# A hybrid decoder step: the samples get a mixer and queries of their own, and every weight split moves to VectorE

## The chip, the core and the metric
The kernel runs on one core of one Trainium2 chip. The metric is the device time of one execution in microseconds (us), the median of three runs. Engines are called as in the profile: PE (TensorE matmul; PEld its weight loads), DVE (VectorE), ACT (ScalarE), POOL (GpSimd), SP (SyncE, which issues transfers). An instruction of an engine starts in the order of that engine's program, when the semaphores it waits for allow it.

## The reference
Two layers over 512 prompt tokens (one sequence) and 64 sample tokens (8 sequences of 8 steps, with state carried in). D is 1024. Each layer is a mixer and an expert retrieval:

```
hn = modulate(rmsnorm(x, norm1), sh1, sc1)          # shift and scale by sequence, from c @ w_ada
xa, bg, cg, xs, ga, gb = split(hn @ w_in, 6)        # six parts of 1024 columns
ya = rglru(conv4(xa)); yb = bg * conv3(cg * xs)     # gated scan over time, short convolution
x += g1 * ((sigmoid(ga) * ya + sigmoid(gb) * yb) @ w_out)
hn2 = modulate(rmsnorm(x, norm2), sh2, sc2)
q = (hn2 @ w_q).reshape(t, 8 heads, 2, 128)
s = einsum('thpd,hpkd->thpk', q, sub_keys)          # 128 scores in each half
sv, si = top_k(s, 16)                               # 16 x 16 sums of a head, of which the best 16:
fv, fi = top_k(sv[:, :, 0, :, None] + sv[:, :, 1, None, :], 16)
idx = si[.., 0] * 128 + si[.., 1] at fi             # one of 16384 experts
g = softmax(fv)
x += g2 * sum_k g_k * gelu(u_tab[idx_k] . hn2) * v_tab[idx_k]
```

Outputs: the normed x of prompt and samples, and the last convolution inputs and scan states. All is float32.

## The kernel before
Channels lie on the partitions, tokens along the free axis: x is 8 channel tiles of 128 x 576, the prompt's 512 columns first. Weights stream as blocks of 128 x 1024 float32 (512 KB), two to a load (`load_pair`, L144, on SP's queue, six raw buffers). To get float32 out of the faster float32r matmuls, each block is cut in two by `split_blk` (L130): ACT copies it to `hi`, and `lo = raw - hi` is a subtraction (L141) on DVE or POOL; four buffers of each. A product is three passes: hi by hi, hi by lo, lo by hi, 24 weight loads for 8 channel tiles. A running sum of `pool_share` decides who subtracts: of the u blocks beside the gates POOL takes all (SHARE_A = 1.0), of the u and v blocks of the product stage every other one (SHARE_B = 0.5), of wq every other one, of w_in and w_out none.

The stages of a layer:
- *Mixer* (`mixer_in`, L342): for each channel tile c six products (`proj`), 48 blocks, over all 576 tokens. Such a product is two matmuls of 256 and 320 columns for each weight load, into the two banks of a `big` tile of PSUM (`mm_tokens`, L152). Convolutions, gates, scan and merge follow on DVE and ACT, in separate operations for prompt and samples. In layer 1 the modulation chunks (`ada`, fp32 matmuls L189) stand between the blocks. Then w_out, 8 blocks.
- *Queries* (`queries`, L663): wq's 16 blocks over all tokens; scores; top-k on DVE (`topk_half`, `combine`).
- *Gates and first activations* (`phase_a`, L774): 384 prompt tokens, the dense ones, meet every expert on PE. Their gates become matrices: DVE writes one-hot rows (`oh`, L794; `A`, L800), PE multiplies them (`pgm`, L805), ACT evicts, and the pieces go to DRAM. Beside this, NA = 80 of the 128 u blocks are multiplied (`pu`, L512); 64 of their activations wait in DRAM (`ad`), 16 in SBUF.
- *Products* (`phase_b`, L844): 128 v blocks are multiplied by activation x gate (`pvo`, L870), and the other 48 u blocks (`ub`) between them. DVE multiplies activation and gate (L900) and splits the result (`wl`, L903).
- *Gathered tokens*: the other 128 prompt tokens and the 64 samples, in NG = 3 groups of 64, fetch their experts' rows by indirect transfers that POOL issues (L520): 192 rows of u and 192 of v a layer, each 128 x 1024. DVE makes a dot of each u row (`ur`, L526) and adds each v row times its weight (`acc`, L543). `pump` emits these steps at rates of the work beside them: 0.3 a us of the queries' vector work, 0.5 of the gates', 1.6 to a block of the products.

The order within an engine is that of a list scheduler: priority is the place in the program, and splits and loads stand AHEAD = 2000 steps before their place (`tc.high_priority`).

Of the kernel before, what the change touches and what calls it, by code (L numbers as in the profile page):

```python
# [1040 lines left out]
```

## Time and profile before

| | |
|---|---|
| device time, three runs | 3845.72, 3853.9, 3854.32 us; median 3853.9 |
| the profiled execution | span 3846.9 us (the page gives no other time of it) |
| PE busy | 3484.8 us, 91% |
| DVE busy | 3204.7 us, 83% |
| POOL busy | 2022.2 us, 53% |
| ACT busy | 1476.0 us, 38% |
| transfers | 960.62 MB, mean 250 GB/s |

Busy shares are means over stages with different limits, so the windows below cut the span at the stages' ends: layer 1's mixer from 42 to 480 us, norm and first queries to 570, queries and gates to 1206, products to 1944; layer 2 the same from 1966 on. An operation's min, median and max show whether it always takes the same time.

### The profile page before, as it was taken

How to read it: one execution, taken by the hardware profiler on the slowest of the kernel's cores; microseconds unless marked ns; L12 is line 12 of the kernel's file. 1: busy time of each engine (PE TensorE's matmuls, PEld its weight loads, DVE VectorE, ACT ScalarE, POOL GpSimd, SP SyncE). 2: the span in 40 equal slices, each digit the busy share in tenths (PEclk: the TensorE clock that was granted, in tenths of full speed). 3: DMA queues.
4: the chain of work that ended last, by engine and by line, in shares of the span. 5: the costliest groups of instructions: out<-in, count | busy, mean ns of one | idle time of the engine just before them, and what ended most of it. 6: DMA issues, size and time to landing. Idle time of an engine off the chain costs nothing.

```text
span 3846.9 us, 57240 instructions
## 1 busy us (share of the span) xinstructions
PE 3484.8 (91%) x21120; PEld 3180.7 (83%) x21120; DVE 3204.7 (83%) x5485; ACT 1476.0 (38%) x1876; POOL 2022.2 (53%) x1360
## 2 busy tenths in 40 slices
PE   8999998776879999999989998987677899999997
PEld 6999988776768999888879998877676799998886
DVE  5444489999997999998875556999999879999888
...
GB/s 249 188 189 165 69 138 263 246 233 223 291 272 298 334 338 340 341 358 362 315 131 79 82 83 65 209 254 233 225 263 279 280 338 322 338 357 342 355 341 200
DMA packets 366712, 960.62 MB, mean 250 GB/s; under 512 B 45920, under 2 KB 149472, under 8 KB 359648
## 3 DMA queue, kind: packets, MB, share of 16 engines
...
q8 instruction: 165, 2.70, 0.3%
...
## 4 chain that ended last, share of the span: by engine, by line
PE 55%; DVE 36%; issue 4%; DMA 2%; POOL 2%; ACT 1%; SPq 0%; DVEq 0%; POOLq 0%; ACTq 0%
PE pvo L870 19%; PE pj L159 16%; PE pu L512 12%; DVE ur L526 11%; DVE oh L794 4%; DVE A L800 4%; PE po L159 3%; POOL vr L520 1%; PE pq L722 1%; PE pm L189 1%; POOL lo_v L141 1%; DVE acc L543 1%; PE pg L420 1%; DMA raw_v<-in_vtab_dram 1%; PE pt L203 1%
## 5 line engine op out<-in xcount | busy, mean ns | idle before, releaser
L520 POOL DMA_INDIRECT ur<-in_utab_dram,gidx x384 | 481.6, 1254 | 512.9 <-DVE dot L526 281.2
L520 POOL DMA_INDIRECT vr<-in_vtab_dram,gidx x384 | 540.8, 1408 | 250.5 <-DVE acc L543 173.4
L543 DVE SCALAR_TENSOR_TENSOR acc<-vr,dot,acc 128x1024 f32<-128x1024 f32 x378 | 644.6, 1705 | 10.6 <-DMA vr<-in_vtab_dram,gidx 7.2
L526 DVE CUSTOM_DVE_ANT_0 ur<-ur,xt 128x1024 f32<-128x1024 f32 x384 | 613.4, 1605 | 8.8 <-DMA ur<-in_utab_dram,gidx 8.8
L512 PE MATMUL pu<-h2h,hi_u 128*128 128x384 f32 x1280 | 454.0, 355 | 62.4 <-ACT ao L830 62.4
L870 PE MATMUL pvo<-hi_v,wh 128*128 128x512 f32 x1536 | 488.7, 392 | 0.0
L870 PE MATMUL pvo<-lo_v,wh 128*128 128x512 f32 x1536 | 477.6, 390 | 0.0
L870 PE MATMUL pvo<-hi_v,wl 128*128 128x512 f32 x1536 | 466.0, 390 | 2.4 <-DVE acc L543 1.2
L512 PE MATMUL pu<-h2h,lo_u 128*128 128x384 f32 x1280 | 452.5, 353 | 6.0 <-POOL lo_u L141 5.9
L512 PE MATMUL pu<-h2l,hi_u 128*128 128x384 f32 x1280 | 451.2, 352 | 0.0
L141 POOL TENSOR_TENSOR lo_u<-raw_u,hi_u 128x1024 fp32r<-128x1024 f32 x160 | 405.6, 2537 | 28.5 <-ACT hi_u L140 25.7
L141 POOL TENSOR_TENSOR lo_v<-raw_v,hi_v 128x1024 fp32r<-128x1024 f32 x128 | 343.8, 2686 | 65.4 <-ACT hi_v L140 63.0
L159 PE MATMUL pj<-hnl,hi_wi 128*128 128x256 f32 (+1 forms) x1536 | 343.1, 301 | 2.5 <-DVE hnl L280 2.4
L159 PE MATMUL pj<-hnh,hi_wi 128*128 128x256 f32 (+1 forms) x1536 | 339.7, 301 | 5.5 <-ACT hnh L283 4.1
L870 PEld LDWEIGHTS pvo<-hi_v,wl 128*128 128x128 f32 x1536 | 288.1, 188 | 64.2 <-DVE wl L903 1.6
L870 PEld LDWEIGHTS pvo<-lo_v,wh 128*128 128x128 f32 x1536 | 288.3, 188 | 61.3
L159 PE MATMUL pj<-hnh,lo_wi 128*128 128x256 f32 (+1 forms) x1536 | 337.7, 298 | 0.0
L870 PEld LDWEIGHTS pvo<-hi_v,wh 128*128 128x128 f32 x1536 | 285.3, 188 | 54.9 <-issue 0.4
L512 PEld LDWEIGHTS pu<-h2h,hi_u 128*128 128x128 f32 x1280 | 256.4, 200 | 65.6 <-ACT ao L830 64.9
L140 ACT ACTIVATE hi_u<-raw_u 128x1024 fp32r<-128x1024 f32 x160 | 169.7, 1061 | 317.0 <-PE pu L512 162.4
L140 ACT ACTIVATE hi_v<-raw_v 128x1024 fp32r<-128x1024 f32 x256 | 272.0, 1062 | 29.5 <-issue 13.8
L512 PEld LDWEIGHTS pu<-h2h,lo_u 128*128 128x128 f32 x1280 | 255.9, 200 | 17.9 <-POOL lo_u L141 13.8
...
## 6 DMA issues: line engine op xcount, KB each, us to landing
raw_v<-in_vtab_dram SPq DMA_DIRECT2D x256, 512.0 KB
raw_u<-in_uT_dram SPq DMA_DIRECT2D x160, 512.0 KB
...
gt<-gd SPq DMA_DIRECT2D x768, 64.0 KB
...
```

Of the source, the lines that this page charges most:

```text
L140: S.activation(hi, raw, AF.Copy)
L141: e.tensor_tensor(out=lo, in0=raw, in1=hi.bitcast(F32), op=ALU.subtract)
L159: PE.matmul(part(out, q), a[:, w], b[:, k, PARTS[q][0]:PARTS[q][1]], start=(k == 0 and a is hi and b is xh), stop=(k == KT - 1 and a is lo))
L189: PE.matmul(pm[j * 32:(j + 1) * 32, 0:256], c32[:, k, :], raw[k // 4][:, j * 256:(j + 1) * 256], start=(k < 4), stop=(k >= 4))
L203: PE.matmul(pt[:, q * 16:q * 16 + NSEQ], ms[:, q * P:(q + 1) * P], sel, start=True, stop=True)
L512: PE.matmul(pu[:, 0:TD], a[:, w], b[:, k, 0:TD], start=(k == 0 and a is hi and b is h2h), stop=(k == KT - 1 and a is lo))
L520: G.indirect_dma_start(out=rt, out_offset=None, in_=tab, in_offset=bass.IndirectOffsetOnAxis(ap=gidx[:, g, h, k:k + 1], axis=0))
L526: V.tensor_tensor_reduce(out=ur, in0=ur, in1=xt[g], scale=1.0, scalar=0.0, op0=ALU.mult, op1=ALU.add, accum_out=dot[:, g, h, k:k + 1])
L543: V.scalar_tensor_tensor(out=acc[g], in0=vr, scalar=w, in1=acc[g], op0=ALU.mult, op1=ALU.add)
L794: V.tensor_tensor(out=o, in0=iota2.unsqueeze(1).to_broadcast([P, 4, P, 2]), in1=slot(t, a, c0), op=ALU.is_equal)
L800: V.tensor_tensor(out=A[:, z], in0=oh[0], in1=slot(t, 2 + z, c0), op=ALU.mult)
L870: PE.matmul(pv[t][q], a[:, tk], b[:, q * 512:(q + 1) * 512], start=(n == 0 and a is wh and b is vh), stop=(n == P - 1 and a is wl))
```

## The change
- The products over all tokens run over the prompt's 512 columns alone, one matmul to a weight load, in one bank (`bank`, four of them).
- The samples get a generator `samples()`. It is stepped 2.5 times (layer 1) or 3 times (layer 2) beside each mixer block (`beside`, SIDE). It makes nine products (six of w_in, w_out, two of wq): the 64 tokens are the stationary operand, plain fp32 weights move in 512 columns, the two column halves to the two halves of the array. For these the weights are streamed a second time in another layout (swin, swout, swq: 72 blocks of 512 KB a layer). Convolution, gates, scan, merge, second norm, top-k and the list of rows follow over all channel tiles at once.
- When the generator is done, the samples' gathers are issued beside the mixer's blocks (MPUMP = 2.5 a block), and go on in the gates. NG falls from 3 to 2; the number of rows is the same. Beside the queries no gather is issued (QRATE 0), beside the gates 0.35 a us (0.5), beside a product block 2.9 while the u blocks run there and 1.0 after (1.6).
- All subtractions of `split_blk` are on DVE. `tc.issue_after(anchor)` puts the gather steps behind the last split in the order; it adds no wait. POOL issues gathers and little else.
- NA falls from 80 to 64: 64 u blocks stand beside the gates, 64 in the product stage; 48 activations wait in DRAM (64).
- Gate pieces are formed in quarters of 4 tokens (halves of 8), so one-hot operations have 512 elements (1024). wh and wl lie in a spare slice of h2h and h2l.
- The mixer's merged output is kept in float32 and split after the loop over c.

```diff
-NG = (T - TD) // 64
-NA = 80
+NG = (NP - TD) // 64
+NA = 64
-SHARE_A, SHARE_B = 1.0, 0.5   # of the splits, what GpSimd takes
-QRATE, ARATE, BPUMP = 0.3, 0.5, 1.6
+SIDE = (2.5, 3.0)
+MPUMP, QRATE, ARATE, BPUMP = 2.5, 0.0, 0.35, (2.9, 1.0)
-    def split_blk(raw, nm, pool_share=0.0):
+    def split_blk(raw, nm):
...
-            e.tensor_tensor(out=lo, in0=raw, in1=hi.bitcast(F32), op=ALU.subtract)
+            anchor[0] = V.tensor_tensor(out=lo, in0=raw, in1=hi.bitcast(F32), op=ALU.subtract).ins
...
-                    for q in qs:
-                        PE.matmul(part(out, q), a[:, w], b[:, k, PARTS[q][0]:PARTS[q][1]],
-                                  start=(k == 0 and a is hi and b is xh), stop=(k == KT - 1 and a is lo))
+                    PE.matmul(out[:, c0:c1], a[:, w], b[:, k, c0:c1],
+                              start=(k == 0 and a is hi and b is xh), stop=(k == KT - 1 and a is lo))
...
+    def pump(n):
+        credit[0] += n
+        while credit[0] >= 1.0 and gtasks:
+            with tc.issue_after(anchor[0]):
+                gtasks.popleft()()
+            credit[0] -= 1.0
+        credit[0] = min(credit[0], 1.0)
...
+        def beside():
+            if todo:
+                n = todo.pop(0)
+                ada(n // 24, [n % 24])
+            steps[0] += SIDE[l]
+            while steps[0] >= 1.0:
+                steps[0] -= 1.0
+                if next(chain, None) is None:
+                    steps[0] = -1e9
+            if steps[0] < -1.0:
+                pump(MPUMP)
...
-            S.activation(mgh[:, c, :], yb, AF.Copy)
-            V.tensor_tensor(out=mgl[:, c, :], in0=yb, in1=mgh[:, c, :].bitcast(F32), op=ALU.subtract)
+        for _ in chain:
+            pass
...
+        def product(src, lhs, nm, put):
+            acc = ubank(f"sa{l}_{nm}")
+            for kk in range(KT // 2):
+                raw = load_pair(src[kk], f"s{l}_{nm}_{kk}")
+                for u in range(2):
+                    k = 2 * kk + u
+                    for r in range(2):
+                        PE.matmul(acc[r * NS:(r + 1) * NS, :], lhs[:, k, :], raw[u][:, r * 512:(r + 1) * 512],
+                                  start=(k == 0), stop=(k == KT - 1))
+                yield 1
+            tm = st.tile([P, 512], F32, tag="rows", bufs=ROWS, name=f"tm{l}_{nm}")
+            S.activation(tm, acc, AF.Copy)
+            pt = small(f"spt{l}_{nm}")
+            for q in range(4):
+                PE.transpose(pt[:, q * P:(q + 1) * P], tm[:, q * P:(q + 1) * P], ident)
+            put(pt)
+            yield 1
...
+        work_of = Gathered(f"s{l}", gidx, gate, dot, {0: xt})
+        work_of.first(0, range(4))
+        work_of.second(1, lambda g, acc: finish_samples(l, mod, acc))
...
-            for half in range(2):
-                pgm = big(f"pgm{l}_{t}_{ch}_{half}")
-                c0 = ch * 16 + half * 8
+            for q in range(4):
+                c0 = ch * 16 + q * 4
...
-                hi, lo = split_blk(raw[u], f"u{l}_{i}", SHARE_A)
+                hi, lo = split_blk(raw[u], f"u{l}_{i}")
...
-                vh, vl = split_blk(vraw[u], f"v{l}_{i}", SHARE_B)
-                wh = pb.tile([P, TD], F32R, tag="wh", bufs=WB, name=f"wh{l}_{i}")
-                wl = pb.tile([P, TD], F32R, tag="wl", bufs=WB, name=f"wl{l}_{i}")
+                vh, vl = split_blk(vraw[u], f"v{l}_{i}")
+                wh, wl = (w_[:, u * TD:(u + 1) * TD] for w_ in (wht, wlt))
...
-                pump(BPUMP)
+                pump(BPUMP[i0 < NA])
```

How the order stands before and after, at three places. First PE's program in layer 1's mixer (`pj` a product of w_in, `sa` one of the samples' products, `spg` their scan gates, `pm` and `pt` the modulation). Before, each weight block meets the tokens in two parts:

```order
L159 MATMUL pj_0_2_615<-hnh,hi_wi_0_2_611 128x256
L159 MATMUL pj_0_2_615<-hnh,hi_wi_0_2_611 128x320
L159 MATMUL pj_0_2_615<-hnl,hi_wi_0_2_611 128x256
L159 MATMUL pj_0_2_615<-hnl,hi_wi_0_2_611 128x320
L159 MATMUL pj_0_2_615<-hnh,lo_wi_0_2_612 128x256
L159 MATMUL pj_0_2_615<-hnh,lo_wi_0_2_612 128x320
```

After, the place between two blocks:

```order
L150 MATMUL pj_1_1_1091<-hnh_334,hi_wi_1_1_1087 128x512
L150 MATMUL pj_1_1_1091<-hnl_335,hi_wi_1_1_1087 128x512
L150 MATMUL pj_1_1_1091<-hnh_334,lo_wi_1_1_1088 128x512
L476 MATMUL sa_gb<-raw_s_gb_1135,hs_511 64x512 x2
L537 MATMUL spg_1_777<-sxc_701,rg_3_1_347 128x64
L186 MATMUL pm_14_1049<-raw_ada_14_1045,c_121 32x256 x4
L186 MATMUL pm_14_1049<-raw_ada_14_1046,c_121 32x256 x4
L476 MATMUL sa_gb<-raw_s_gb_1136,hs_511 64x512 x2
L200 MATMUL pt_13_1060<-sel,ms_13_972 128x9 x2
L476 MATMUL sa_cg<-raw_s_cg_1155,hs_511 64x512 x2
L186 MATMUL pm_15_1120<-raw_ada_15_1116,c_121 32x256 x4
```

The pairs became single matmuls of 512 columns, and the samples' products, with the weights as the moving operand, stand between them.

Second, the gates. POOL's program before, where u blocks 50 to 54 are split (`ur` a gather):

```order
L141 TENSOR_TENSOR lo_u_50_10278<-raw_u_25_10272,hi_u_50_10277 128x1024
L520 DMA ur_0_2_7_10625<-in_utab_dram,gidx_4952 128x1024
L520 DMA ur_0_2_8_10787<-in_utab_dram,gidx_4952 128x1024
L141 TENSOR_TENSOR lo_u_51_10308<-raw_u_25_10273,hi_u_51_10307 128x1024
L520 DMA ur_0_2_9_10813<-in_utab_dram,gidx_4952 128x1024
L520 DMA ur_0_2_10_10907<-in_utab_dram,gidx_4952 128x1024
L141 TENSOR_TENSOR lo_u_52_10402<-raw_u_26_10396,hi_u_52_10401 128x1024
L141 TENSOR_TENSOR lo_u_53_10432<-raw_u_26_10397,hi_u_53_10431 128x1024
L520 DMA ur_0_2_11_10935<-in_utab_dram,gidx_4952 128x1024
L520 DMA ur_0_2_12_10943<-in_utab_dram,gidx_4952 128x1024
L141 TENSOR_TENSOR lo_u_54_10526<-raw_u_27_10520,hi_u_54_10525 128x1024
```

DVE's program after, from the split of block 53 on (`smd`, `ggd`, `t8d`, `eqd` belong to the combination of the top-k lists):

```order
L133 TENSOR_TENSOR lo_u_53_9821<-raw_u_26_9787,hi_u_53_9820 128x1024
L805 TENSOR_TENSOR eqd_2_6219<-eqd_2_6219,doff 128x2048
L819 TENSOR_SCALAR smd_2_6209<-smd_2_6209 128x8
L794 TENSOR_TENSOR t8d_2_6220<-eqd_2_6219 128x1024
L820 TENSOR_TENSOR ggd_2_6141<-exd_2_6208,smd_2_6209 128x128
L795 TENSOR_TENSOR t8d_2_6220<-t8d_2_6220 128x128x4
L809 TENSOR_TENSOR eqd_2_6219<-eqd_2_6219,dsid_2_6214 128x2048
L903 CAST ghd_2_6143<-ggd_2_6141 128x128
L796 TENSOR_TENSOR t8d_2_6220<-t8d_2_6220 128x128x2
```

and 245 rows later the next split, among the one-hots:

```order
L930 TENSOR_TENSOR oh_2_36_8961<-iota_83,sl_2_4302 128x512
L935 TENSOR_TENSOR A_2_36_8965<-oh_2_36_8961,sl_2_4302 128x512 x2
L930 TENSOR_TENSOR oh_2_40_8981<-iota_83,sl_2_4302 128x512
L133 TENSOR_TENSOR lo_u_54_9855<-raw_u_27_9850,hi_u_54_9854 128x1024
L930 TENSOR_TENSOR oh_2_40_8983<-iota_83,sl_2_4302 128x512
L935 TENSOR_TENSOR A_2_40_8985<-oh_2_40_8981,sl_2_4302 128x512 x2
L930 TENSOR_TENSOR oh_2_44_9000<-iota_83,sl_2_4302 128x512
L930 TENSOR_TENSOR oh_2_44_8998<-iota_83,sl_2_4302 128x512
L935 TENSOR_TENSOR A_2_44_9002<-oh_2_44_8998,sl_2_4302 128x512 x2
L133 TENSOR_TENSOR lo_u_55_9885<-raw_u_27_9851,hi_u_55_9884 128x1024
```

The splits moved from POOL's own list, where they alternate with gathers, into DVE's, where splits 53 and 54 are 245 rows apart.

Third, DVE in the product stage at block 92, before (`ao` activation by gate, `wl` its lower part, `ur` and `dot` a gathered dot):

```order
L141 TENSOR_TENSOR lo_ub_92_12336<-raw_ub_88_2_12330,hi_ub_92_12335 128x1024
L526 ISA ur_2_3_3_14779,dot_4954<-ur_2_3_3_14779,xt_2_5542 128x1024
L526 ISA dot_4954 128x1
L900 TENSOR_TENSOR ao_90_12174<-ao_90_12174,gt_88_12235 128x384 x2
L526 ISA ur_2_3_4_14782,dot_4954<-ur_2_3_4_14782,xt_2_5542 128x1024
L526 ISA dot_4954 128x1
L526 ISA ur_2_3_5_14812,dot_4954<-ur_2_3_5_14812,xt_2_5542 128x1024
L526 ISA dot_4954 128x1
L903 TENSOR_TENSOR wl_90_12404<-ao_90_12174,wh_90_12403 128x384
L141 TENSOR_TENSOR lo_v_90_12400<-raw_v_88_1_12395,hi_v_90_12399 128x1024
L526 ISA ur_2_3_6_14846,dot_4954<-ur_2_3_6_14846,xt_2_5542 128x1024
```

and after (`urp` a prompt token's row; `h2l` now holds what wl held):

```order
L133 TENSOR_TENSOR lo_ub_92_12136<-raw_ub_88_2_12130,hi_ub_92_12135 128x1024
L1032 TENSOR_TENSOR ao_90_11975<-ao_90_11975,gt_88_12036 128x384
L667 ISA urp_0_2_0_12093,dot_4299<-urp_0_2_0_12093,xt_0_4756 128x1024
L667 ISA dot_4299 128x1
L133 TENSOR_TENSOR lo_ub_93_12166<-raw_ub_88_2_12131,hi_ub_93_12165 128x1024
L1032 TENSOR_TENSOR ao_90_11975<-ao_90_11975,gt_88_12036 128x384
L667 ISA urp_0_2_1_12096,dot_4299<-urp_0_2_1_12096,xt_0_4756 128x1024
L667 ISA dot_4299 128x1
L1035 TENSOR_TENSOR h2l<-ao_90_11975,h2h 128x384
L133 TENSOR_TENSOR lo_v_90_12200<-raw_v_88_1_12195,hi_v_90_12199 128x1024
L667 ISA urp_0_2_2_12124,dot_4299<-urp_0_2_2_12124,xt_0_4756 128x1024
L667 ISA dot_4299 128x1
```

Every block now has its subtraction here (`lo_ub_93`, `lo_v_91`, where every other one was POOL's), and gathered dots stand right behind the splits.

## Rows read from the trace of the kernel before
**Rows 1.** The page's first lines: span, then busy us, share, instructions by engine
```profile
span 3846.9 us, 57240 instructions
...
PE 3484.8 (91%) x21120; PEld 3180.7 (83%) x21120; DVE 3204.7 (83%) x5485; ACT 1476.0 (38%) x1876; POOL 2022.2 (53%) x1360
```
**Rows 2.** The page: the chain that ended last, shares by engine
```profile
PE 55%; DVE 36%; issue 4%; DMA 2%; POOL 2%; ACT 1%; SPq 0%; DVEq 0%; POOLq 0%; ACTq 0%
```
**Rows 3.** Windows: stretch, its us, busy us (instructions) by engine, PEclk, DMA share, GB/s
```profile
42.00:480.00 438.00, 436.27 (x3447) 405.37 (x3448) 208.65 (x392) 176.70 (x248) 23.56 (x78) 0.99 0.48 156
480.00:570.00 90.00, 82.91 (x648) 74.06 (x647) 76.22 (x311) 37.12 (x68) 29.25 (x21) 0.91 0.35 121
570.00:1206.00 636.00, 494.11 (x3146) 467.86 (x3147) 621.70 (x1363) 239.84 (x255) 400.00 (x237) 0.87 0.77 259
1206.00:1944.00 738.00, 736.76 (x3539) 644.70 (x3538) 662.61 (x630) 274.92 (x365) 548.18 (x315) 1.00 0.95 339
1700.00:1800.00 100.00, 100.00 (x450) 82.78 (x449) 85.31 (x94) 37.05 (x48) 65.03 (x39) 1.00 1.00 362
1966.00:2352.00 386.00, 379.55 (x2753) 374.43 (x2753) 210.34 (x360) 169.59 (x218) 37.14 (x83) 0.98 0.24 77
2440.00:3075.00 635.00, 490.45 (x3136) 463.12 (x3135) 621.25 (x1360) 239.07 (x253) 397.93 (x237) 0.88 0.77 258
```
**Rows 4.** Waits from 570 to 1206 us: in total, times, longest
```profile
PE pgm L805 <- DVE A L800: 53.0, 49, 3.4
```
**Rows 5.** Lines, 570 to 1206: busy us, mean ns | idle before, releasers
```profile
L526 DVE CUSTOM_DVE_ANT_0 ur<-ur,xt 128x1024 f32<-128x1024 f32 x153 | 245.0, 1605 | 4.8 <-DMA ur<-in_utab_dram,gidx 4.8
...
L141 POOL TENSOR_TENSOR lo_u<-raw_u,hi_u 128x1024 fp32r<-128x1024 f32 x80 | 202.9, 2538 | 14.4 <-ACT hi_u L140 13.0
...
L805 PE MATMUL pgm<-A,oh 128*128 128x128 f16 x768 | 72.7, 250 | 53.1 <-DVE A L800 53.0
```
**Rows 6.** Each line's instructions: ns min/median/max, first and last start, forms
```profile
L543 DVE SCALAR_TENSOR_TENSOR acc<-vr,dot,acc x378: 1186/1277/3974, 1336.1 to 3815.1; 128x1024 f32<-128x1024 f32 x189
...
L526 DVE CUSTOM_DVE_ANT_0 ur<-ur,xt x384: 1192/1212/4065, 569.7 to 3198.4; 128x1024 f32<-128x1024 f32 x192
...
L141 POOL TENSOR_TENSOR lo_u<-raw_u,hi_u x160: 2346/2407/4423, 618.9 to 3069.7; 128x1024 fp32r<-128x1024 f32 x160
...
L141 DVE TENSOR_TENSOR lo_wi<-raw_wi,hi_wi x96: 1197/1224/1226, 36.2 to 2274.9; 128x1024 fp32r<-128x1024 f32 x96
...
L794 DVE TENSOR_TENSOR oh<-iota,sl x192: 674/681/5640, 960.0 to 3052.1; 128x1024 f16<-128x1024 f16 x192
```
**Rows 7.** Timeline of DVE at 3142 us: start, duration, instruction
```profile
3142.36 1.21 DVE L526 CUSTOM_DVE_ANT_0 ur<-ur,xt 128x1024 f32<-128x1024 f32 x1
...
3143.50 3.40 DVE L526 CUSTOM_DVE_ANT_0 ur<-ur,xt 128x1024 f32<-128x1024 f32 x1
...
3146.83 1.21 DVE L526 CUSTOM_DVE_ANT_0 ur<-ur,xt 128x1024 f32<-128x1024 f32 x1
```
**Rows 8.** Timeline of POOL over the same stretch
```profile
3142.91 2.91 POOL L141 TENSOR_TENSOR lo_v<-raw_v,hi_v 128x1024 fp32r<-128x1024 f32 x1
3145.96 1.77 POOL L520 DMA_INDIRECT ur<-in_utab_dram,gidx  x1
```
**Rows 9.** The chain in order of time: start, us, engine, product, line, matmuls
```profile
1186.88 49.14 PE pu L512 x283
1256.62 8.34 PE pu L512 x48
...
2035.88 38.39 PE pj L159 x288
...
3625.22 122.07 PE pvo L870 x538
```
**Rows 10.** Timeline of PE at two fp32 products of the mixer
```profile
203.83 1.07 PE L189 MATMUL pm<-raw_ada,c 128*32 128x256 f32 x16
...
2114.43 2.10 PE L420 MATMUL pg<-xc,rg 128*128 128x256 f32 x8
```

More of the change, by code (lines that the diff above doesn't have):

```diff
@@ L150, in load_pair, with mm_tokens @@
         return raw
-    def mm_tokens(out, hi, lo, xh, xl, halves=((0, 1),)):
-        for qs in halves:
+    def mm_tokens(out, hi, lo, xh, xl, parts=((0, NP),)):
+        for c0, c1 in parts:
             for k in range(KT):
@@ L359, in mixer_in, with work, load_rg @@
         SY.dma_start(bb, bufb[l])
-        def work(c, nm):
-            if nm == "yb":
-                return mx.tile([P, T], F32, tag=nm, bufs=1, name=f"{nm}{l}_{c}")
-            tag, n = ("xt", NG) if nm in ("sga", "sgb", "h") else ("rows", ROWS)
-            return st.tile([P, T], F32, tag=tag, bufs=n, name=f"{nm}{l}_{c}")
+        def work(nm, shape=(NP,)):
+            return mx.tile([P, *shape], F32, tag="w", bufs=WORK, name=f"{nm}{l}")
+        def load_rg(c, pair):
+            for t_, d_ in zip(pair, (rgwa, rgwx)):
+                for h in range(2):
+                    SY.dma_start(t_[h * 64:(h + 1) * 64, h * 64:(h + 1) * 64], d_[l, h][:, c, :])
+        chain = samples(l, vt, mod, mx, A, B, work, load_rg, rgs[2:], (ba, hz, bb), (ca_o, h_o, cb_o))
+        steps = [0.0]
+        def beside():
[9 more added lines that the diff above has]
+                pump(MPUMP)
         todo = list(range(8, 48 - NB)) if l == 0 else []
@@ L370, in mixer_in @@
             rga, rgx = rgs[c % 2]
[L371 to L373 removed]
+            load_rg(c, rgs[c % 2])
             def proj(g):
@@ new lines, in finish_samples @@
+    def finish_samples(l, mod, acc):
+        pf = small(f"pfs{l}")
+        for k in range(KT):
+            PE.matmul(pf[:, k * 64:(k + 1) * 64], acc[:, k * P:(k + 1) * P], eye2, start=True, stop=True)
+        tmp = st.tile([P, KT, SB, ST], F32, tag="rows", bufs=ROWS, name=f"fin{l}")
+        V.tensor_tensor(out=tmp, in0=pf.rearrange("p (k b t) -> p k b t", k=KT, b=SB),
+                        in1=per_seq(mod[:, 5 * KT:6 * KT, 1:NSEQ]), op=ALU.mult)
+        V.tensor_tensor(out=x[:, :, NP:T], in0=x[:, :, NP:T], in1=tmp.rearrange("p k b t -> p k (b t)"), op=ALU.add)
+        all_squares(NP, NS, st.tile([P, KT, P], F32, tag="rows", bufs=ROWS, name=f"sqs{l}"))
@@ L534, in peer @@
-            acc = {}
-            def vsum(g, h, k):
-                vr = rows_of(vtab, "vr", (g, h, k))
-                w = dot[:, g, h, k:k + 1]
-                if h == 0 and k == 0:
-                    acc[g] = st.tile([P, D], F32, tag="xt", bufs=NG, name=f"acc{l}_{g}")
-                    V.tensor_scalar(out=acc[g], in0=vr, scalar1=w, scalar2=None, op0=ALU.mult)
-                else:
-                    V.scalar_tensor_tensor(out=acc[g], in0=vr, scalar=w, in1=acc[g], op0=ALU.mult, op1=ALU.add)
@@ L627, in combine @@
         V.tensor_copy(pf, fi.rearrange("p h k -> p (h k)"))
-        eqpr = pool.tile([P, 2, n, 16], F16, tag="wide", bufs=bufs, name=f"eq{nm}")
+        if wide_pool is None:
+            eqpr = pool.tile([P, 2, n, 16], F16, tag="wide", bufs=bufs, name=f"eq{nm}")
+        else:
+            eqpr = wide_pool.tile([P, 2, n, 16], F16, tag="rows", bufs=ROWS, name=f"eq{nm}")
         eq, pr = eqpr[:, 0], eqpr[:, 1]
@@ new lines, in queries @@
+                h = m // 2
+                ii = pq.tile([P, NG, 16], F32, tag="ii", bufs=1, name=f"iig{l}_{h}")
+                jj = pq.tile([P, NG, 16], F32, tag="jj", bufs=1, name=f"jjg{l}_{h}")
+                combine(pq, svg[:, :, m - 1:m + 1, :], sig[:, :, m - 1:m + 1, :], NG, f"g{l}_{h}",
+                        work_of.gate[:, :, h, :], ii.rearrange("p g k -> p (g k)"), jj.rearrange("p g k -> p (g k)"),
+                        tick)
+                V.scalar_tensor_tensor(out=jj, in0=ii, scalar=float(P), in1=jj, op0=ALU.mult, op1=ALU.add)
@@ L753, in queries @@
+                V.tensor_scalar(out=work_of.gidx[:, :, h, :], in0=jj, scalar1=float(l * NEXP), scalar2=None, op0=ALU.add)
+                for g in range(NG):
+                    work_of.first(g, (h,))
             for u in range(2):
@@ L924, in phase_b @@
                                            scalar=g2[:, k, 0:1], in1=x[:, k, cols], op0=ALU.mult, op1=ALU.add)
[L925 to L931 removed]
+            all_squares(t * P, P, sq[:, 2 if t else 0])
     decay = decay_rates()
```

596 lines of the change are left out of this document (322 added, 274 removed).

## The prediction
> **What bounds the kernel now.** I read the page's busy times first: PE 91% and DVE 83% of the span of 3846.9 us [rows 1]. Neither says where a change pays, so next came the chain that ended last: PE 55%, DVE 36% [rows 2]. Two engines, then, each in stretches of its own. The windows show which [rows 3]. In the mixer (42 to 480, and 1966 to 2352 in layer 2) and in the product stage (1206 to 1944) PE is busy for all but 1 to 7 us: these stages cost what their matmuls cost. From 480 to 1206 (queries, top-k, gate matrices, 80 u blocks) it is DVE that is full: 621.70 of 636 us between 570 and 1206, while PE has 494.11 and its granted clock averages 0.87. Layer 2 repeats it (621.25 of 635). PE waits there for DVE's one-hots, 53.0 us in 49 waits [rows 4]. So work given to DVE is dear between 480 and 1206 and nearly free elsewhere; work given to PE is dear everywhere else.
>
> **Why DVE is full there** decides this case. A gathered dot on DVE, two inputs of 1024, takes 1.21 us in the median and 4.07 at most; a weighted sum 1.28 and 3.97; a one-hot 0.68 and 5.64 [rows 6]. The timeline at 3142 shows what makes the difference: a dot of 1.21 us and, straight behind it, one of 3.40, which lies over a split on POOL from 3142.91 to 3145.82 [rows 7, 8]. The next dot starts while POOL is issuing a gather (3145.96, 1.77 us) and takes 1.21. It is POOL's splits that stretch DVE, by 3.40 - 1.21 = 2.19 us apiece, not its gathers. The split itself takes 1.22 us on DVE, 2.41 on POOL [rows 6]. Handing one to POOL costs DVE more than doing it. Starts of successive dots lie 1.14 us apart, which I use for splits and gather steps alike.
>
> **The change, part by part** (per layer unless said).
>
> *Mixer and w_out.* 56 blocks of 24 weight loads. Before, a load serves 256 + 320 columns: 38.39 us for 288 matmuls is 266.6 ns a pair. After, it serves 512 columns, which is the shape of a pvo matmul: 122.07/538 = 226.9 ns [rows 9]. 56 x 24 x 39.7 ns = -53. The samples come back as nine fp32 products of eight tiles, two column halves side by side, 512 columns, two passes: 9 x 8 x 2 x 512 = 73,728 column passes. No such product stands in the trace. The modulation's fp32 product takes 1.07 us for 2 rounds x 2 passes x 256 columns in four column quarters, 1.04 ns a column; the gates' takes 2.10 us for 2304, 0.91 ns [rows 10]. So 67 to 77 us; from below, at the split passes' 226.9/512 = 0.44 ns, it would be 33. I take 70, since both fp32 rows are near it, and 10 for transposes, sample gates and scores. Net +27; bounds -10 to +35. DVE's extra work (the samples' vector operations and early gathers, about 70 us) hides behind PE: DVE is busy 209 of 438 there.
>
> *The mixer's transfers.* 9 x 8 x 512 KB = 38 MB of extra weight copies and 64 gathers of 512 KB, 34 MB, join the 156 GB/s x 438 us = 68 MB of layer 1: 140 MB in 465 us is 300 GB/s mean, and the weight copies come first. The most that a stretch shows is 362 [rows 3]. I put +30 on layer 1 (bounds 0 to 60) and +10 on layer 2, which stands at 77 GB/s.
>
> *Queries and gates, 480 to 1206.* DVE before: 76.22 + 621.70 = 698 us. Gone: the stretch of 88 POOL splits (80 of u [rows 5], 8 of wq by the code's share of one half), 88 x 2.19 = -193; of 153 gather dots [rows 5] 95 that now stand beside the mixer and the products, x 1.14 = -108. New: 72 more splits on DVE x 1.14 = +82; one-hots in twice as many halves of the size, some +13; the samples' own top-k and combine leave, -35. Sum 457, about 86 of it beside the queries. PE: the queries' 16 blocks x 24 x 226.9 ns = 87, with scores and transposes about 122; 64 u blocks x 24 x 8.34/48 us [rows 9] = 267; gate products some 50. The order does not let these overlap freely: the first 54 u splits stand among about 215 us of DVE work, their matmuls with gate products are about 240 on PE, so PE sets that part at 245 with some waiting. Then 245 rows of combines and one-hots, about 110 us, come before split 54. PE has the matmuls of two blocks in hand (-8) and otherwise little but gate products (72.7 us for a layer's 768 at the low clock [rows 5]). The last ten blocks are 42 us of PE alone. 15 + 122 + 245 + 102 + 42 = 526, and I take 536 for waits behind gather rows: -190 from 726. If the clock stays at its lower level after the idle stretch, the 42 become 84; but 283 matmuls from 1186.88 on took 49.14 us [rows 9], full speed right behind the gates, so I give it nothing and keep the 42 in the range.
>
> *Product stage.* 16 more u blocks met here: 16 x 24 x 8.34/48 = +67, the same work that left the gates. DVE: 663 [rows 3], less 88 POOL splits x 2.19 = -193, 104 more splits +119, 26 more gather steps +30, the rest some +20: 640 of about 805, still below PE. Since a gather step now stands in DVE's queue behind a split, a row that lands late would hold the next split, and through it PE; DVE has about 165 us of slack over 128 blocks, 1.3 us a block, before that costs. Bounds -5 (waits that exist now go) and +60; I take +10. The reloads fall from 64 to 48 blocks, which offsets the extra transfers: 339 GB/s of mean now, 326 to 359 after by bytes over time, close under 362.
>
> *Other edits* (scales kept, memsets hoisted, split of the merged product after the loop, copies on ACT): ACT is busy 38% and has room; the late split of the merged product leaves PE bare for one tile, under 5 us, inside the bounds of the mixer.
>
> *Sum* against the profiled execution: 3846.9 + 2 x 27 + 30 + 10 - 2 x 190 + 2 x (67 + 10) = 3715. The page gives that execution no time but its span, and the median of the runs is 7.0 above it, so 3722 against 3853.9.
>
> One rule I weighed against this. The lock on DVE's second input, says the Trainium skill ("SBUF — State Buffer", section "Who interferes with whom"), is with any GpSimd instruction that reads SBUF; issuing a gather reads its indices there. If gathers held DVE as splits do, only part of the stretch would go, and the second rival below would be the forecast. The dot of 1.21 us beside the issue of a gather [rows 7, 8] speaks against it.
>
> **Rivals.**
> (1) *The splits starve PE (slower).* Before, POOL cuts u blocks whatever DVE does. After, each waits its turn behind combines and gather steps, with four buffers of split weights between. I assumed that of the 215 us ahead of the long run almost all lies beside PE. If 100 of it lies bare, the stage takes about 630 and saves 96: 3715 + 2 x 94 = 3903, 3910 against the median. It decides from a saving of 124 a layer downward (stage over 602), where the sum is 3847. For it: the long run of 245 rows shows that the order does not level DVE's work. Against: DVE's sum ahead of it is under PE's, so a lump has to exceed two blocks, 8 us, to bite.
> (2) *Half of the relief.* If gathers and waits, not the splits, make half of the stretch, DVE keeps 97 us more in the stage and the stage saves 93 to 110: about 3890. For it: dots and one-hots reach 4 and 5.6 us, more than one split explains. Against: rows 7 and 8.
> (3) *More than forecast.* No DMA stall in the mixer (-40), no waits in the products (-20), a stage of 515 (-42): 3620. For it: DVE has slack in all PE-bound stages, and the granted clock there is 0.95 to 1.00 already.
> (4) *Transfers set the pace* in layer 1's mixer and in the products: +60 more in all, 3785. For it 1.00 of DMA share at 362 GB/s between 1700 and 1800 with PE busy for 100.00 of 100 us [rows 3]; the same row says that PE did not wait even so.
>
> **How the numbers follow.** Forecast 0.53, (3) 0.15, (4) 0.10, (1) 0.15, (2) 0.07. A measurement of this kernel can tell about 0.3%, 11.6 us, from no change. Faster: the forecast's, (3)'s and (4)'s, 0.78; rivals (1) and (2) end mostly above 3865, some within: slower 0.17, same 0.05. Range 3620 to 3870: down to (3), up past (4) to where (1) starts to decide; the far halves of (1) and (2) and the depth below (3) are left out.
>
> **What would show it.** Dots and weighted sums at means of 1.21 and 1.28 us, not the 1.6 of the dots now [rows 5], or the reading of the stretch is wrong. Layer 1's stretch from the first query to the first product block at 515 to 540 us with a gap of about 100 us in PE towards its end; over 600 is rival (1) if DVE's operations are short, (2) if they stay long. Product stage 800 to 820 with PE full; idle PE at v blocks would be late gather rows. Mixer 460 to 500 in layer 1, 410 to 425 in layer 2, each product of the samples 7 to 8.5 us. The prediction fails outright if the gates' stage keeps more than 600 us.

## The result and the profile after

The changed kernel takes 3763.2 us (median of four runs, 3755.13 to 3771.79), the kernel before 3850.4 beside it: a ratio of 0.977, 95% interval 0.976 to 0.979. The forecast was 3722, range 3620 to 3870. The profiled execution has a span of 3759.6 us, 87 less than before.

The page's busy times, to be laid beside [rows 1]:

```profile
PE 3533.5 (94%) x18606; PEld 2936.9 (78%) x18606; DVE 2965.1 (79%) x6160; ACT 1494.4 (40%) x2032; POOL 1037.8 (28%) x830
```

DVE executes 675 instructions more and is busy 240 us less. Where that comes from is in the durations of single lines, min/median/max in ns, the answer to [rows 6]:

```profile
L683 DVE SCALAR_TENSOR_TENSOR accp<-vrp,dot,accp x252: 1270/1279/1322, 1510.3 to 3720.5; 128x1024 f32<-128x1024 f32 x126
...
L667 DVE CUSTOM_DVE_ANT_0 urp<-urp,xt x256: 1207/1218/1226, 1161.7 to 3288.4; 128x1024 f32<-128x1024 f32 x128
...
L930 DVE TENSOR_TENSOR oh<-iota,sl x384: 410/417/469, 934.7 to 2921.5; 128x512 f16<-128x512 f16 x192
```

Medians are those of before (the one-hot is half as wide); the tails are gone. The longest dot took 4065 ns and takes 1227 (a sample's; 1226 in the row of the prompt's dots above), although POOL still issues 768 gathers.

The stages, in the columns of [rows 3]: mixer with w_out, queries and gates, products, of layer 1 and then layer 2, with the gap between the layers:

```profile
40.00:576.00 536.00, 491.19 (x2597) 332.50 (x2598) 301.52 (x591) 188.19 (x284) 77.77 (x64) 0.94 0.74 263
576.00:1116.00 540.00, 493.51 (x3062) 434.13 (x3062) 490.11 (x1584) 263.30 (x340) 80.65 (x63) 0.88 0.60 216
1116.00:1910.00 794.00, 793.89 (x3870) 702.45 (x3869) 656.83 (x840) 287.74 (x389) 331.84 (x252) 1.00 0.94 336
1910.00:1948.00 38.00, 15.66 (x82) 13.56 (x80) 26.61 (x49) 10.41 (x17) 8.29 (x15) 0.64 0.31 107
1948.00:2405.00 457.00, 423.01 (x1893) 298.61 (x1892) 310.68 (x571) 174.51 (x247) 98.36 (x75) 0.97 0.69 239
2405.00:2933.00 528.00, 488.81 (x2997) 432.65 (x2996) 487.25 (x1583) 260.72 (x335) 70.23 (x62) 0.88 0.58 210
2933.00:3728.00 795.00, 793.14 (x3858) 701.05 (x3857) 647.91 (x830) 285.54 (x386) 365.77 (x247) 1.00 0.90 328
```

| stage | forecast, layers 1, 2 | measured |
|---|---|---|
| mixer and w_out | +57, +37 | +96, +71 |
| queries and gates | -190, -190 | -186, -195 |
| products | +77, +77 | +56, +57 |
| gap between the layers, end | 0, 0 | +16, -2 |
| sum | -132 | -87 |

The gates came out as forecast and the mixers did not. The 16 u blocks that moved to the products (67 us) are there in full, too: the cut at 1206 us leaves 52 matmuls of the gates' last u blocks, about 9 us, in the product stage of before, a third of them in this row of its stretch from 1206 to 1944:

```profile
L512 PE MATMUL pu<-h2h,lo_u 128*128 128x384 f32 x18 | 6.0, 334 | 0.0
```

The changed kernel has none behind its cut at 1116, so that by the same cut layer 1's products are some 66 us longer and the gates some 195 us shorter. In the gates the long run of combines and one-hots shows, as PE at half its clock more than as idle time:

```profile
576.00:916.00 340.00, 328.64 (x1930) 304.31 (x1930) 318.82 (x1157) 137.93 (x210) 80.65 (x63) 0.98 0.70 243
916.00:936.00 20.00, 5.23 (x27) 4.07 (x26) 18.83 (x35) 3.83 (x5) 0.00 (x0) 0.66 0.25 96
936.00:1036.00 100.00, 81.44 (x547) 52.60 (x547) 97.65 (x274) 71.47 (x68) 0.00 (x0) 0.50 0.40 169
1036.00:1056.00 20.00, 18.20 (x115) 16.75 (x114) 12.78 (x31) 11.20 (x14) 0.00 (x0) 0.76 0.35 132
1056.00:1116.00 60.00, 60.00 (x451) 56.40 (x449) 42.03 (x90) 38.87 (x45) 0.00 (x0) 1.00 0.56 209
```

Up to 916 PE is busy nearly throughout. Then it is busy for 5 of 20 us, and from 936 to 1036 the granted clock is 0.50, the lower of its two levels (1.2 of 2.4 GHz), with DVE busy for 98 of 100 us. From 1056 on, with u blocks to multiply, PE is busy throughout and the clock is 1.00, although one-hots are still being written (the last one starts at 1104).

### The profile page after: what moved, and what is told of

The parts are those of the page before. It is cut to its first block, busy times and chain, and to the rows that moved or that the text cites. A ratio compares the mean times of both kernels' runs of the same rounds, so it can differ in the third digit from the quotient of the medians.

```text
span 3759.6 us, 52675 instructions
## 1 busy us (share of the span) xinstructions
PE 3533.5 (94%) x18606; PEld 2936.9 (78%) x18606; DVE 2965.1 (79%) x6160; ACT 1494.4 (40%) x2032; POOL 1037.8 (28%) x830
## 4 chain that ended last, share of the span: by engine, by line
PE 48%; issue 15%; POOL 9%; DVE 9%; DMA 3%; ACT 1%; SPq 1%; POOLq 0%; ACTq 0%; DVEq 0%
PE pu L712 21%; PE pvo L1003 13%; PE pq L857 5%; POOL vrp L661 4%; POOL urp L661 4%; PE pj L150 3%; DVE A L935 3%; DVE oh L930 2%; POOL urs L661 2%; PE po L150 1%; DMA gt<-gd 1%; DMA raw_wi<-in_win_dram 1%; PE pgm L940 1%; PE pd L871 1%; DMA vrp<-in_vtab_dram,gidx 1%
## 5 line engine op out<-in xcount | busy, mean ns | idle before, releaser
L661 POOL DMA_INDIRECT urp<-in_utab_dram,gidx x256 | 366.3, 1431 | 600.5 <-DVE dot L667 467.5
L1003 PE MATMUL pvo<-hi_v,h2h 128*128 128x512 f32 x1536 | 487.7, 390 | 0.1
L661 POOL DMA_INDIRECT vrp<-in_vtab_dram,gidx x256 | 346.5, 1353 | 511.8 <-DVE accp L683 470.5
L1003 PE MATMUL pvo<-lo_v,h2h 128*128 128x512 f32 x1536 | 475.8, 389 | 0.0
L1003 PE MATMUL pvo<-hi_v,h2l 128*128 128x512 f32 x1536 | 465.6, 390 | 0.2 <-DVE h2l L1035 0.2
L712 PE MATMUL pu<-h2h,lo_ub 128*128 128x384 f32 x1024 | 343.1, 335 | 1.7 <-DVE lo_ub L133 1.6
L712 PE MATMUL pu<-h2h,hi_ub 128*128 128x384 f32 x1024 | 342.7, 335 | 0.0
L712 PE MATMUL pu<-h2l,hi_ub 128*128 128x384 f32 x1024 | 342.5, 334 | 0.0
L150 PE MATMUL pj<-hnh,hi_wi 128*128 128x512 f32 (+1 forms) x800 | 319.9, 401 | 18.7 <-ACT hi_wi L132 10.0
L683 DVE SCALAR_TENSOR_TENSOR accp<-vrp,dot,accp 128x1024 f32<-128x1024 f32 x252 | 322.7, 1281 | 6.1 <-DMA vrp<-in_vtab_dram,gidx 4.9
```

The source lines that it names most:

```text
L150: PE.matmul(out[:, c0:c1], a[:, w], b[:, k, c0:c1], start=(k == 0 and a is hi and b is xh), stop=(k == KT - 1 and a is lo))
L661: G.indirect_dma_start(out=rt, out_offset=None, in_=tab, in_offset=bass.IndirectOffsetOnAxis(ap=self.gidx[:, g, h, k:k + 1], axis=0))
L683: V.scalar_tensor_tensor(out=self.acc[g], in0=vr, scalar=w, in1=self.acc[g], op0=ALU.mult, op1=ALU.add)
L712: PE.matmul(pu[:, 0:TD], a[:, w], b[:, 0:NT, k, :], start=(k == 0 and a is hi and b is h2h), stop=(k == KT - 1 and a is lo))
L1003: PE.matmul(pv[t][q], a[:, tk], b[:, q * 512:(q + 1) * 512], start=(n == 0 and a is wh and b is vh), stop=(n == P - 1 and a is wl))
```

## The experiments

Theory: POOL's splits stretch DVE's operations, so that moving them to DVE frees it where it is full. Rivals: it is the smaller load of that stage that pays (fewer gathers, fewer u blocks), or splits in DVE's queue starve PE. Each kernel ran beside the kernel before on one chip; ratios are to that. The median of the kernel before was 3848.6 to 3850.8 on the four chips, so that times of different sets can be compared to some 2 us.

**The splits back on POOL, the rest as changed (e1)**, with `pool_share` 1.0 for u, 0.5 for ub, v and wq, 0 elsewhere.

```diff
-            anchor[0] = V.tensor_tensor(out=lo, in0=raw, in1=hi.bitcast(F32), op=ALU.subtract).ins
+            turn[0] += pool_share
+            if turn[0] >= 1.0:
+                turn[0] -= 1.0
+                G.tensor_tensor(out=lo, in0=raw, in1=hi.bitcast(F32), op=ALU.subtract)
+            else:
+                anchor[0] = V.tensor_tensor(out=lo, in0=raw, in1=hi.bitcast(F32), op=ALU.subtract).ins
```

> The changed kernel with the splits shared out as before (all u blocks beside the gates, every other block of the products and of wq to POOL), everything else as changed. If POOL's splits stretch DVE by 2.19 us apiece and a DVE split costs 1.14, 72 splits in queries and gates give DVE about 75 us more there, the stage goes from 528 to 540 us to about 580 to 615 a layer, dots and sums go from 1.22 and 1.28 us back to about 1.6, the product stage stays within 20 us of 794 because DVE still has room: 3840 to 3930 us in all. Rival (the gain comes from moving gathers and u blocks out of the stage, and it is the same who splits): within 15 us of 3763, or faster, since POOL feeds PE without waiting its turn on DVE.

Measured 3881.2, ratio 1.008 (1.006 to 1.010): 118 us slower than the change, and 0.8% slower than before. The same two kinds of line, in ns, in e1:

```profile
L690 DVE SCALAR_TENSOR_TENSOR accp<-vrp,dot,accp x252: 1268/1277/4185, 1569.8 to 3838.3; 128x1024 f32<-128x1024 f32 x126
...
L674 DVE CUSTOM_DVE_ANT_0 urp<-urp,xt x256: 1208/1214/3946, 1215.7 to 3396.5; 128x1024 f32<-128x1024 f32 x128
```

and its gates and products in layer 1:

```profile
578.00:1171.00 593.00, 497.63 (x3062) 441.64 (x3061) 542.49 (x1511) 258.99 (x342) 261.19 (x136) 0.87 0.56 196
1171.00:1967.00 796.00, 794.52 (x3874) 702.76 (x3873) 700.79 (x745) 290.62 (x387) 593.92 (x347) 1.00 0.94 335
```

The tails return, and 53 of the 118 us are layer 1's gates (540 to 593). DVE has 72 splits less in that stretch, 72 x 1.14 = 82 us of work, and is busy 52 us more: 134/72 = 1.9 us of stretch a split, under the 2.19 of the forecast, over the 1.14 that a split costs on DVE. Layer 2's gates take 56 us more (584 for 528). Layer 1's products, PE-bound, take 2 us more. So the rival on the load falls for the whole kernel. For the gates' stage alone it does not: at 593 us it is still 133 shorter than before (726), by the gather steps and u blocks that left it. But in e1 the mixers and products cost more than that saves.

**The kernel before with the splits on DVE, alone (e2), and with the tie (e5).**

```diff
-SHARE_A, SHARE_B = 1.0, 0.5   # of the splits, what GpSimd takes
+SHARE_A, SHARE_B = 0.0, 0.0   # of the splits, what GpSimd takes
-                hi, lo = split_blk(raw[u], f"wq{l}_{hp}", 0.5)
+                hi, lo = split_blk(raw[u], f"wq{l}_{hp}", 0.0)
...                                              # e5 also:
-                    gtasks[gpos[0]]()
+                    with tc.issue_after(anchor[0]):
+                        gtasks[gpos[0]]()
```

> The kernel before with every split on DVE and nothing else changed. If the stretch is POOL's splits' alone, DVE's sum between 480 and 1206 falls by 88 x 1.05 = 92 us a layer, the stage takes 610 to 650 us, the products stay PE-bound at 738: 3650 to 3720 us, so this one part would give more than the whole change. Rival (splits on DVE starve PE, since they wait behind gathers and top-k): the stage stays at 726 or grows, 3850 us or more; if a POOL split cost DVE nothing, 88 x 1.14 = 100 us more a layer, about 4050.

Measured 4035.2, ratio 1.048 (1.046 to 1.050), the wrong side of the expectation. Yet DVE is busy 2949.7 us, 255 less than before, with 352 more splits: (255 + 352 x 1.14)/352 = 1.9 us of stretch a split again. The theory of the cost stands; the time was lost elsewhere. Windows of e2:

```profile
480.00:1282.00 802.00, 564.72 (x3809) 533.44 (x3808) 767.75 (x1930) 278.07 (x325) 433.75 (x299) 0.81 0.85 303
800.00:900.00 100.00, 100.00 (x579) 100.00 (x578) 98.60 (x321) 40.33 (x54) 38.24 (x32) 1.00 0.93 331
900.00:1000.00 100.00, 12.02 (x63) 10.45 (x61) 94.78 (x212) 6.65 (x9) 72.49 (x51) 0.57 0.86 290
1000.00:1100.00 100.00, 29.55 (x226) 23.40 (x227) 96.99 (x143) 27.47 (x16) 72.73 (x47) 0.50 0.90 316
```

PE was not starved at first (100 of 100 us at 800); it ran through its u blocks and then stood while DVE worked off gather steps ahead of the one-hots: 69 dots between 900 and 1033, and the first one-hot at 1030 (960 before). 281 gather steps stand between 480 and 1282, 153 between 480 and 1206 before, 128 x 1.2 us more in the one stage where DVE is the bound. Why the scheduler moved them there is not shown; a guess is that it found them ready sooner with POOL less loaded. e5 takes that away:

> The kernel before with every split on DVE, as in e2, and now each gather step queued behind the last split on DVE (order only). In e2 283 gather steps stood between 570 and 1290, where the kernel before has 153, and the one-hots came only from 1033 on. If it is this hoisting that cost e2 its gain, the tie brings the count back to about 150, the stage from 480 goes from 802 to 620 to 670 us, products 740 to 760: 3680 to 3780. Rival (splits in DVE's queue starve PE whatever the gathers do): 3950 or more.

Measured 3941.9, ratio 1.024 (1.022 to 1.027). The stage falls a little more than expected, the total does not:

```profile
480.00:1095.00 615.00, 553.31 (x3790) 523.03 (x3790) 567.67 (x1674) 283.44 (x327) 159.77 (x126) 0.91 0.70 253
1095.00:1829.00 734.00, 734.00 (x3525) 643.23 (x3524) 546.87 (x701) 266.87 (x358) 241.02 (x174) 1.00 0.87 300
1829.00:1923.00 94.00, 14.75 (x79) 12.46 (x77) 76.83 (x89) 10.00 (x14) 60.22 (x54) 0.55 0.85 294
1923.00:2402.00 479.00, 387.28 (x2766) 380.76 (x2767) 275.79 (x413) 170.49 (x220) 103.45 (x130) 0.88 0.34 114
...
3749.00:3940.00 191.00, 20.44 (x98) 17.74 (x96) 148.87 (x153) 10.07 (x14) 118.90 (x95) 0.53 0.79 277
```

The stage falls from 726 to 615 us with 109 gather steps in it. The products hold 173, and 99 of the 384 are left for after them, with PE idle: in layer 1 half of them run in the gap and half in what should be layer 2's mixer, and the two take 573 us where before took 408; in layer 2 they stand at the end, 191 us for 34. The tie alone moves the loss behind the products.

**The change without the tie (e6)**, `pump` calling `gtasks.popleft()()` without `tc.issue_after`:

> The changed kernel without the tie: gather steps go where the scheduler's priorities put them. If the tie keeps gather steps out of the stretch where DVE is full, then without it more of them stand between the first query and the first product block (55 a layer now) at 1.2 us apiece, the gates grow by 80 to 150 us a layer as in e2: 3900 to 4050. Rival (the emission rates alone set their place): within 15 us of 3763.

Measured 3952.0, ratio 1.026 (1.023 to 1.029). Layer 1 hardly moves (the gates take 544 us for 540); layer 2 does, from 528 and 795:

```profile
2399.00:3068.00 669.00, 476.55 (x2881) 424.36 (x2880) 646.12 (x1813) 248.76 (x323) 255.97 (x218) 0.79 0.79 279
3068.00:3922.00 854.00, 810.39 (x3992) 713.04 (x3990) 497.42 (x611) 304.95 (x405) 121.83 (x91) 0.97 0.63 217
```

213 gather steps stand in layer 2's stage, 57 with the tie. It is the order that keeps DVE free there.

**The mixer: weights once (e3; its samples' products are then not the reference's), no gathers (e4).**

```diff
-                raw = load_pair(src[kk], f"s{l}_{nm}_{kk}")          # e3
+                if kk == 0:
+                    raw = load_pair(src[kk], f"s{l}_{nm}_{kk}")
-MPUMP, QRATE, ARATE, BPUMP = 2.5, 0.0, 0.35, (2.9, 1.0)              # e4
+MPUMP, QRATE, ARATE, BPUMP = 0.0, 0.0, 0.35, (2.9, 2.3)
```

> The changed kernel, but each of the samples' nine products loads one pair of weight blocks instead of four and uses it for all eight tiles (so the samples' products are not the reference's); the matmuls stay. 27 of 36 pairs a layer, 28 MB, are not loaded. If the mixer's excess over the forecast is waiting for weight transfers and the lower clock that follows, PE's idle time in the two mixers (45 and 34 us) mostly goes, and the time falls by 60 to 100 us, to 3665 to 3700. Rival (the excess is the work itself, and waits for operations on DVE and ACT): within 15 us of 3763.

> The changed kernel with no gather beside the mixer's blocks (rate 0 for 2.5) and 2.3 for 1.0 gather steps beside each block of the products' second half, so that 64 more stand in the product stage. If gathers collide with the weight transfers in the mixer's second half, the mixers fall by 15 to 30 us each, the gates keep their number of steps, the products have room on DVE (657 of 794 busy): 3710 to 3750. Rival (gathers in the mixer are free, and more of them in the products stop PE there through DVE or transfers): mixer unchanged, products 10 to 60 us longer, 3780 to 3880.

e3: 3733.4, ratio 0.969 (0.967 to 0.971). The mixers lose 19 and 10 us and the total 30, half of the least that was expected: between the two theories. e4: 3914.2, ratio 1.016 (1.014 to 1.018). Its mixers, and what follows layer 1's products:

```profile
40.00:538.00 498.00, 477.42 (x2595) 325.50 (x2595) 231.34 (x463) 186.40 (x281) 0.00 (x0) 0.98 0.63 216
...
1870.00:1992.00 122.00, 4.03 (x18) 3.49 (x16) 92.97 (x81) 0.00 (x0) 92.06 (x69) 0.51 0.88 307
2016.00:2453.00 437.00, 419.12 (x1892) 298.94 (x1893) 231.66 (x436) 174.36 (x248) 1.83 (x8) 0.98 0.47 162
```

The mixers are 38 and 20 us shorter, above the expected 15 to 30 in layer 1; but the gather steps that left them did not fit into the products at 2.3 a block (252 stand there, 251 in the changed kernel), and DVE worked them off for 122 us after the last product. A step beside the mixer costs 58 us / 138 steps = 0.4 us.

**How the gates are filled: 80 u blocks (e7), fewer gathers (e8), both paced anew (e10).**

```diff
-NA = 64                       # e7 and e10
+NA = 80
-... ARATE, BPUMP = ... 0.35, (2.9, 1.0)
+... ARATE, BPUMP = ... 0.35, (2.9, 1.4)      # e7
+... ARATE, BPUMP = ... 0.1, (2.9, 1.65)      # e8
+... ARATE, BPUMP = ... 0.5, (2.9, 1.5)       # e10
```

> The changed kernel with 80 u blocks beside the gates (64 of the activations in DRAM, as before), 48 in the products, and 1.4 for 1.0 gather steps a block in the products' second half, so that their number stays. The products lose 16 x 24 x 173.8 ns = 67 us a layer. If the gates have room on PE (busy 373 of 408 only at a granted clock of 0.85) they grow by 20 to 45 us: 3670 to 3730. Rival (the order leaves PE bare in the long run of one-hots, and the added blocks come before or after it): gates 60 to 75 us longer, 3750 to 3790.

> The changed kernel with 0.1 for 0.35 gather steps a us beside the gates, and 1.65 for 1.0 beside each block of the products' second half: about 40 steps a layer move. If DVE bounds the gates, these 40 x 1.2 us leave that stage (540 and 528 to 490 to 500) and the products take them (657 of 794 busy) with up to 20 us more at their end: 3690 to 3740. Rival (gathers in the products' second half are bound by their transfers, 2.5 us a step as in e4's tail): products' ends 40 to 60 us later, 3760 to 3800.

e7: 3769.8, ratio 0.979 (0.977 to 0.981), in the rival's range, though not by its mechanism. Layer 1 of e7:

```profile
579.00:1146.00 567.00, 542.96 (x3444) 489.75 (x3443) 509.90 (x1600) 283.69 (x372) 81.89 (x63) 0.93 0.63 225
1146.00:1873.00 727.00, 727.00 (x3489) 635.97 (x3488) 599.32 (x794) 265.55 (x357) 291.79 (x221) 1.00 0.94 337
1873.00:1960.00 87.00, 15.75 (x82) 13.54 (x80) 65.16 (x77) 9.36 (x14) 43.12 (x41) 0.57 0.66 232
```

The gates take 27 us more and the products 67 less, as expected; a gap of 87 us for 38, because 39 gather steps were left over, takes it back. e8: 3798.6, ratio 0.986 (0.984 to 0.989), inside its rival's range: 42 us less in the gates (498), 66 more in the gap (104). 42 steps left the stage, 57 to 15, and 48 were left over where 9 had been: 1.0 us a step in the gates, 66/39 = 1.7 after the products.

The products take no more steps than that, whatever is asked: 251 in the changed kernel, 252 in e4, 254 in e8, in 794 us each time, at 336 or 337 GB/s, with DVE at work for 655 to 659 us. That is about 0.32 a us, and in e7 they take 221 in 727, 0.30. Whether the transfers or the five buffers for rows set this was not tested.

> The kernel e7 (changed, 80 u blocks beside the gates) with 0.5 for 0.35 gather steps a us beside the gates and 1.5 for 1.4 beside the products' second half. In e7 the products lost 67 us a layer and the gates gained 28, but the last prompt rows came 63 and 34 us after the last product. About 25 steps more in the gates cost 30 us there, and take 25 x 2.8 us off the tail: 3735 to 3765. Rival (the transfers of the products bound the tail and DVE the gates, so that the steps cost the same wherever they stand): 3765 to 3790.

e10: 3727.7, ratio 0.968 (0.965 to 0.970), better than expected. With 81 steps in layer 1's stage for e7's 57 the gap is 41 us again, and the stage 591.

**The kernel before, splits on DVE, tied and repaced (e9)**: e5 with ARATE 0.6 and BPUMP (3.2, 1.7), for the products' first and second half.

> The kernel e5 (before, every split on DVE, gather steps tied behind them) with the steps repaced: 0.6 for 0.5 a us beside the gates, and 3.2 and 1.7 for 1.6 beside a product block in its first and second half. In e5 the stage fell from 726 to 615 us, but with 109 steps in it and 173 in the products 99 of 384 were left for after the last product block, 94 us in layer 1 and 191 at the end. If only their pace is wrong, about 130 steps stand in the stage (640 us), 240 to 250 in the products (734 to 760 us at 340 GB/s), a tail of 20 to 40 us: 3690 to 3740, under the changed kernel, and the samples' own mixer is not what pays. Rival (the products' transfers are full, 300 GB/s of 362 with 173 steps, so that 75 more stretch them): products 770 us and a tail of 60 to 90 us, 3780 to 3850; then the 64 to 74 steps that the change has beside the mixer are what it needs.

Measured 3728.3, ratio 0.969 (0.966 to 0.971). Layer 1:

```profile
480.00:1108.00 628.00, 551.26 (x3790) 521.44 (x3791) 586.27 (x1704) 280.34 (x325) 182.75 (x142) 0.90 0.72 261
1108.00:1843.00 735.00, 735.00 (x3535) 644.25 (x3535) 618.10 (x752) 268.93 (x361) 318.30 (x233) 1.00 0.95 342
1843.00:1866.00 23.00, 10.38 (x63) 8.87 (x61) 22.00 (x40) 8.47 (x12) 9.11 (x12) 0.78 0.73 234
1866.00:2290.00 424.00, 387.81 (x2770) 381.30 (x2771) 233.25 (x380) 170.26 (x220) 60.99 (x97) 0.93 0.28 88
...
3655.00:3720.00 65.00, 14.85 (x83) 12.85 (x81) 50.75 (x70) 7.96 (x11) 22.59 (x19) 0.60 0.61 207
```

125 steps stand in the stage and some 231 in the products, at 342 GB/s. The tails are short but not gone: 27 steps are left behind layer 1's products, where gap and mixer take 447 us for 408 before, and 23 at the end, which takes 65 us for 34. Even so this kernel, which has no mixer of the samples' own, beats the change by 35 us.

**The row copies of the modulation in buffers of their own (e11)**, on e10: in the mixer `ms` comes from a tag of its own with two buffers, not from `rows`.

> The kernel e10 with the modulation's row copies (ms) in two buffers of their own in the mixer, not in the pool that the gathered rows use. In layer 1's mixer ACT waits 43 us in 7 waits for a gathered dot to free a row buffer for ms, and PE 12.6 us for ms, and the granted clock falls to 0.77 around the first gathers (352 to 404 us). If that is how the gathers cost layer 1's mixer 38 us, it shortens by 10 to 20 us there, layer 2 (no modulation in it) stays: 3708 to 3718. Rival (gathers and weights contend for transfers alone): within 6 us of 3728.

Measured 3715.5, ratio 0.966 (0.964 to 0.967), the fastest here. Waits in the changed kernel's first mixer, and its clock around the first gathers:

```profile
ACT ms L192 <- DVE dots L667: 43.3, 7, 17.6
...
PE pt L200 <- ACT ms L192: 12.6, 4, 8.5
```

```profile
352.00:404.00 52.00, 38.36 (x215) 26.55 (x215) 34.76 (x65) 15.13 (x24) 21.54 (x20) 0.77 0.89 332
```

The same stretch in e11:

```profile
352.00:404.00 52.00, 46.86 (x259) 33.99 (x261) 37.83 (x86) 20.16 (x29) 15.71 (x14) 0.93 0.82 291
```

Layer 1's mixer goes from 542 to 527 us. So some 15 of the 38 us that gathers cost there were a shared buffer pool: a gathered row held the buffer that a small copy in PE's path needed.

## Why the prediction was right or wrong

The time came out at 3763 for 3722. Part of that closeness is cancellation: the two mixers took 73 us more than forecast and the two product stages 41 less.

- *The stretch of DVE by POOL's splits*: right in kind, shown by e1 and e2, and the dots and sums came back to the 1.22 and 1.28 us announced. Its size was 1.9 us a split, not 2.19; over 88 splits that is 26 of the 33 us by which DVE's work in the stage (490) exceeds the forecast's 457.
- *Queries and gates, -190*: -186 and -195. The order of events is the one forecast, but its parts are not, and that their sum held is in part luck: 340 us up to where PE runs dry (forecast 15 + 122 + 245 = 382), 140 of PE dry or at half its clock (102), 60 of PE full again (42, with 10 for waits). The gap of about 100 us in PE came as 100 us at the lower clock, busy for 81, rather than as idle time. Rival 1 (starving) and rival 2 (half of the relief) are not what happened.
- *Which edit does it*: the prediction gave the tie no price, as order without a wait. That was the gap in it, and the forecast held because the change has the tie. The same splits on DVE without it cost 185 us on the kernel before (e2), and the change without it is 189 us slower (e6).
- *Mixer and w_out, net +27, and its transfers, +30 and +10*: the step that failed. With no gathers beside it PE's work is 41 and 40 us above before (e4: 477.42 against 436.27, 419.12 against 379.55). The nine products have the price I took:

```profile
L476 PE MATMUL sa_wq<-raw_s_wq,sh 128*64 128x512 f32 x64 | 15.7, 605 | 2.5 <-DMA raw_s_wq<-in_swq_dram 2.5
...
L476 PE MATMUL sa_xa<-raw_s_xa,hs 128*64 128x512 f32 x32 | 8.4, 600 | 0.0
```

  Their eight groups in layer 1 add up to 74 us busy, and 70 was the forecast. What is short is the prompt's gain: with 70 and 10 us for the samples, 41 more in all leaves it at about -39, not -53. Most of the difference lies where PE changes from one product to another, which the forecast put at nothing. PE in e4:

```profile
179.55 0.60 PE L476 MATMUL sa_xs<-raw_s_xs,hs 128*64 128x512 f32 x2
180.08 0.50 PE L150 MATMUL pj<-hnh,hi_wi 128*128 128x512 f32 x1
180.42 0.40 PE L150 MATMUL pj<-hnl,hi_wi 128*128 128x512 f32 x1
180.65 0.39 PE L150 MATMUL pj<-hnh,lo_wi 128*128 128x512 f32 x1
```

  The first matmul of w_in ends 0.43 us after the samples' product, the next ones 0.24 and 0.22 us after each other. In layer 1 of e4 68 such matmuls of w_in stand behind another product, 0.38 us in the mean for 0.227: about 10 us. That two blocks of w_in and two of w_out still go in two parts costs little: a pair of 256 columns takes 0.240 us for 0.227, 96 times, about 1 us. (A load for each pair, as the prediction has it, is not what the rows show: there are as many loads as matmuls, before too, 3448 beside 3447 in [rows 3]. The price of the pair, 266.6 ns, was measured and stands.) The rest of the miss is the gathers: 38 and 20 us (e4), on top of 19 and 10 for the weight copies (e3), against 30 and 10 for both; each was left out by itself, and no run leaves out both. The mixers of 536 and 457 us lie outside the 460 to 500 and 410 to 425 announced. I had counted bytes; what the gathers cost was partly a shared buffer (e11), and then the clock, 0.94 in that mixer and 0.98 without them.
- *Products, +77*: +56 and +57, or about +66 by the same cut (see the stages). The 67 us are there; the margin of 10 for late rows was not needed. That rival 4 speaks of 3785 where its sum, 3722 + 60, is 3782 changes nothing.
- *The samples' own path*: not weighed as a whole. It lengthens the mixers by 96 and 71 us and leaves 64 and 74 gather steps there. e9 without it and e10 with it, both with 80 u blocks and paced anew, are level at 3728, and e9 is still 39 and 31 us longer than before behind its products, where rows are left. The 12 us between e10 and e11 come from one buffer. So no run shows that this path pays: splits on DVE, the tie and the pacing give as much without it. How far either kernel could still be paced was not run.
